# One diffusion step on one core: the low parts, the second Fourier pass and the modulation units moved between stages

## Chip, core and metric

The kernel runs on one core of a Trainium2 chip, as one launch. The metric is the device time of one execution in microseconds; lower is better. Five engines run their own instruction streams in order and wait for one another by semaphores: PE (TensorE, matrix products), ACT (ScalarE), DVE (VectorE), POOL (GpSimd) and SP (SyncE, which only issues transfers here).

## The reference, cut

One layer of a hybrid network is computed for 128 context tokens and 256 latent tokens (T = 384 columns in all), model width D = 2048, in float32:

```python
mod = jax.nn.silu(cond) @ lw['w_ada'] + lw['b_ada']            # 6 modulation vectors
h = rmsnorm(x, norm_pre_mix) * (1.0 + sc1) + sh1
proj = h @ lw['w_in']                  # q, k, v, output gate g, decay factors, Fourier groups fo
o = GLA(q, k, v, decays)               # 4 heads, chunks of 64, two directions
o = (o * rsqrt(mean(o * o)) * gla_out_norm * silu(g))
f = jnp.fft.fft2(fg, axes=(1, 3), norm='ortho').real           # 4 groups of 256 channels
gates = jax.nn.sigmoid(h @ lw['w_gate'] + lw['b_gate'])
merged = g_a * (o @ lw['w_br_gla']) + g_b * (f @ lw['w_br_four'])
m = merged @ lw['w_out']
x = x + ga1 * rmsnorm(m, norm_post_mix)
h = rmsnorm(x, norm_pre_ffn) * (1.0 + sc2) + sh2
ff = (silu(h @ w_ffn_gate) * (h @ w_ffn_up)) @ w_ffn_down
x = x + ga2 * rmsnorm(ff, norm_post_ffn)
```

## The kernel before

**Numbers in two parts.** PE multiplies in a rounded float32 format. To keep float32 accuracy each weight and each activation is split into a high part (the rounded value) and a low part (the rest), and each product is three matmuls: high with high, high with low, low with high. Weights come from HBM in granules of 128 rows by 1024 columns (512 KB). For each granule `load` issues the transfer into a `raw` buffer on SP's queue, and `split` makes the two parts: ACT casts `raw` to `whi` (lines 290, 293, 299, the same cast at three places), and then DVE subtracts, `wlo = raw - whi` (line 286). Four buffers of each part exist; granules are split about three ahead of their use. `grab` takes the next finished granule and then pushes one more load and split into the streams. The instructions of PE, ACT, DVE and POOL stay in the order in which the program is written; SP's transfers are ordered by a scheduler.

**Stages.** In order: the v projection with the first normalisation (to about 150 us); q, k and the first 25 of 32 branch-gate columns, with the GLA heads woven in (to 440 us); the last 7 gate columns with the Fourier channel transform woven in, the folding stage (to 544 us); the 8 output gates with the DFT over positions and the first Fourier projections woven in (to 665 us); the 16 GLA branch projections with the remaining Fourier projections (to 745 us); `w_out` (to 880 us); and the FFN. One 128-column projection is two halves, each 24 matmuls on one granule (`proj`, line 325).

**Work at the side.** After each half `proj` steps a side generator once. In the GLA stage (`side` at the GLA stage) that is one step of `gla` and one of the modulation; in the folding stage one turn of `run_after`; among the output gates one unit of modulation, one step of the DFT and one of the Nyquist weights.

**Modulation units.** The modulation vectors 2 to 4 come from `ada_rest`. One unit takes one 128 x 1024 block of `w_ada` (`adaw`, loaded on POOL's queue, two buffers) and adds it, scaled by one column of the conditioning for each of the two token kinds, to `adacc`: two DVE instructions (lines 704 and 706). Where `on_pe` is set, the unit is four matmuls into `pr` on PE instead (line 696). After 16 units of a vector half come a step without work, a step in which eight matmuls collect `adacc` into `pr` (line 717) and ACT copies it to `adev`, and a step in which PE transposes that into `ptm` (line 670) and DVE writes `mods`. What is left after the `w_out` column KT-4 is drained at once. `ada` is the same generator, slowed or quickened by `rate`. `TAIL` names the GLA branch projections that carry a unit, and whether it runs on PE.

**The folding stage.** It has 14 turns, one after each half. `ends` n adds mirrored token columns (DVE t, line 725; four r, lines 730 and 731; ACT casts the high part), `parts` n writes the low part of that (hF, line 737), and an `f` is one granule of Fourier columns against the folded activations: 16 matmuls into `pfo` (lines 1036 and 1037). Its granule is first combined in place by two DVE instructions (`fold_across`, raw, lines 255 and 256); such a granule's low part already waits until the next split (`low_due`), that of a gate granule follows its own cast at once. There are two passes of eight `f` each, for two pairs of groups; each pass fills four of the five PSUM buffers named `side`, and ACT and DVE copy the first pass's sums out (X, lines 1043 and 1044).

**The Fourier projections.** `four` i (17 matmuls into `pf`, lines 1233 to 1236) takes a granule of `w_br_four` that DVE first folds into `ws` (lines 243 and 244); its result is evicted by ACT (fd), combined by DVE (fd, y), multiplied by its gate and stored to DRAM, from where the GLA branch projection of the same column reads it back. In the stage of the output gates one `four` stands between the two halves of columns 3 to 7, and one after most columns. `gcol` finishes a column: three transposes (pt), ACT gs, DVE gs, ACT o_hi, DVE o_lo.

Of the kernel before, what the change touches and what calls it, by code (L numbers as in the profile page):

```python
# [22 lines left out]
KT = D // P  # L23
# [14 lines left out]
XU = 2  # L38
GF = 25
GD = 256  # L40
TAIL = {2: True, 5: True, 8: True, 11: False, 12: True, 13: False, 14: False}


C_TRI = 0
# [63 lines left out]
def tile_step(ctx: ExitStack, tc: tile.TileContext, a, o):  # L108
# [57 lines left out]
    turns = 2 * (32 - GF)  # L166
    after = [[] for _ in range(turns)]
    for n in range(8):
        at = n + n // 4
# [1 line left out]
        after[at + 1].insert(0, ("parts", n))  # L171
        after[at + 3].insert(0, ("f", 0, n))
    for n in range(8):
        after[turns - 1 - (7 - n + 1) // 4].append(("f", 1, n))
    across = set()
    for at, todo in enumerate(after):
        srcs.append(a["w_gate"][GF + at // 2, at % 2])
# [6 lines left out]
    fourier = iter(range(KT))  # L184
    mix_order = []
    between = [[] for _ in range(8)]
    for i in range(8):
        mix_order.append(("o", i))
        if i > 2:
            between[i].append(next(fourier))  # L190
            mix_order.append(("b", between[i][0]))
        mix_order += [("b", next(fourier)) for _ in range((i > 1) + (i == 7))]
    for i in range(KT):
        mix_order.append(("a", i))
        if i in (1, 4, 7, 9):
            mix_order.append(("b", next(fourier)))
    folded = set()
    for b, i in mix_order:
# [46 lines left out]
        return ws.rearrange("p i g c -> p (i g c)")  # L245

    folded_due = []
    low_due = []
    crossed = iter(range(KT))
    wq = const.tile([P, KT, 4], F32, name="wq")  # L250
# [12 lines left out]
    def split(at=None, eng=DVE, defer=None):  # L263


        if raws:
            raw, pairs, spare = raws.pop(0)
            if spare and depth[0] > 2:
                spare_raws.append(spare)
            if pairs == 2:  # L270
                fold_across(raw)
            while low_due:
                low_due.pop()()
            hi, lo = (
                p.tile([P, G], F32R, tag=t, name=n, bufs=b)
                for n, (p, t, b) in zip(("whi", "wlo"), at or ((wp, "whi", 4), (wp, "wlo", 4)))
            )
            for cast, _ in folded_due:
                cast()
            while folded_due:  # L280
                folded_due.pop()[1]()
            if pairs == 1:
                raw = fold(raw)

            def low():
                eng.tensor_sub(lo, raw, hi.bitcast(F32))  # L286
                ready.append((hi, lo))

            if pairs == 2:
                ACT.copy(hi, raw)  # L290
                low_due.append(low)
            elif pairs:
                folded_due.append((lambda: ACT.copy(hi, raw), low))
            elif defer is not None:
                ACT.copy(hi, raw)
                defer.append(lambda: eng.tensor_sub(lo, raw, hi.bitcast(F32)))
                ready.append((hi, lo))
            else:
                ACT.copy(hi, raw)  # L299
                low()  # L300

    def push():
        if not depth[0]:
# [57 lines left out]
    def catch_up():  # L361
        while later:
            later.pop()()
# [318 lines left out]
    on_pe = [False]  # L682
# [69 lines left out]
    with ExitStack() as s:  # L752
# [25 lines left out]
        def gla():  # L778
# [10 lines left out]
            for h in range(NH):  # L789
# [9 lines left out]
                for d in range(2):  # L799
                    s0.append(pg.tile([P, 1, DV], F32, tag=f"s0{d}", name="s0"))  # L800
                    SP.dma_start(s0[d], a["s0"][d, h])
                yield
                qin, kin, kcr, kout, dec = [], [], [], [], []

                z = [pss.tile([P, n, 2, P], F32, tag="side", name="z") for n in (2, 1)]
# [15 lines left out]
                split_act(lah, lal, la)  # L821
                yield
                if h == 0:
                    yield
                    yield
                for d in range(2):

# [138 lines left out]
        def side():  # L966
            while True:
                next(gl, None)
                next(ada, None)
                yield  # L970

        sd = side()
        for i in qk_order[1:]:
            proj(psm, hT, keep(qk, i), sd)

# [36 lines left out]
    with ExitStack() as s:  # L1012
# [33 lines left out]
        def run_after():  # L1046
            for at, todo in enumerate(after):
                for what, *n in todo:
                    if what == "ends":
                        ends(*n)  # L1050
                    elif what == "parts":
                        over_parts(2 * n[0], folds.pop(n[0]), True)
                    else:
                        if n == [1, 5]:
                            depth[0] = 2
                            spare_raws.clear()
                        across_n(*n)
                if at == turns // 2:
                    SP.dma_start(cd, a["consts"][:, C_CE:NC])
                if at == turns - 1:  # L1060
                    next(ada, None)
                yield

        ra = run_after()
        for i in range(GF, 32):
            proj(psm, hT, gate(more, i), ra)
            if i == GF:
                depth[0] = 4
                spare_raws.extend([lambda: more.tile([P, G], F32, tag="raw3", name="raw3", bufs=2)] * 2)
        catch_up()  # L1070
        depth[0] = 0
        xq = px.tile([P, HT], F32, name="xq")
        POOL.memset(xq, 0.0)
# [14 lines left out]
    with ExitStack() as s:  # L1088
# [84 lines left out]

        def side():
            while True:
                on_pe[0] = turn[0] > 5 and turn[0] % 2
                turn[0] += 1
                next(ada, None)
                on_pe[0] = False
                next(df, None)  # L1180
                next(nw, None)
                yield
# [71 lines left out]
        for b, i in mix_order:  # L1254
            if b == "o":
                if i == 1:
                    gate_of()
                proj(psm, hT, lambda p, i=i: gcol(p, i), sd, [lambda n=n: four(n) for n in between[i]])
                if i == 1:
                    gate_of()  # L1260
                continue
            if b == "b":
                if not i:
                    for g in (df, nw):
                        for _ in g:
                            pass
                    depth[0] = 4
                    spare_raws.extend([
                        lambda: px.tile([P, G], F32, tag="wr", name="raw3"), lambda: px.tile([P, G], F32, tag="cd", name="raw3"),
                    ])  # L1270
                if not any(i in x for x in between):
                    four(i)
            else:
                catch_up()
                if mT is None:
                    mT = alloc_A()
                if i == KT - 4:
                    depth[0] = 2
                    spare_raws.clear()
                if i in TAIL:  # L1280
                    on_pe[0] = TAIL[i]
                    next(ada, None)
                    on_pe[0] = False
                p = psm.tile([P, T], F32, tag="mm", name="pmm")
                w = grab()
                while unstored:
                    unstored.pop()()
                gemm(p, w, oT, 8)
                g, y = gates.pop((b, i))
                DVE.tensor_mul(g, g, p)  # L1290
                DVE.tensor_add(y, y, g)
                if late:
                    split_act(*late.pop())
                late.append((mT[0][:, i, :], mT[1][:, i, :], y))
                gate_of()
# [797 lines left out]
```

## Time and profile before

| what | value |
| --- | --- |
| time, median of 3 runs | 1955.1 us (1954.99 to 1955.59) |
| the profiled execution | 1954.77 us, of which its span 1953.0 us |
| busy in it: PE, DVE, ACT | 1924.9, 1653.2, 915.8 us |
| PE without work in the span | 28.1 us |
| mean granted TensorE clock | 0.997 |

The span runs from the first to the last recorded instruction; the other 1.8 us lie around it. A row of the timeline gives the start, the duration, the engine, the line and operation, output and inputs, and in brackets how long the engine sat idle before it and what ended that. A row of the windows gives, for a stretch of the span, its length and the busy time of PE, PE's weight loads, DVE, ACT and POOL with their instruction counts, then the granted clock, the DMA share and GB/s. PE sums overlapping matmuls only once, so a stretch in which PE is busy throughout still can be slower than another.

### The profile page before, as it was taken

The page shows a single profiled execution, that of the slowest core. Times are in us where ns is not written, and L with a number is a line of the kernel's source. Part 1 is how long each engine was busy: PE and PEld are TensorE (multiplying, and loading weights), DVE is VectorE, ACT ScalarE, POOL GpSimd, SP SyncE. Part 2 cuts the span into 40 slices and gives each one's busy share as a digit, 9 for nine tenths or more (in the row PEclk, how much of TensorE's full clock was granted, in tenths as well). Part 3 has the DMA queues.
Part 4 walks back from the last instruction along what each step waited for, and adds up shares of the span by engine and source line. Part 5 has one row for each costly group of instructions (what it writes and reads, how often), then busy time and mean ns, then how long its engine had stood idle before and what let it go on. Part 6 is the DMA issues. An engine that isn't in the chain of part 4 may idle for free.

```text
span 1953.0 us, 27519 instructions
## 1 busy us (share of the span) xinstructions
PE 1924.9 (99%) x10518; PEld 1693.6 (87%) x10518; DVE 1653.2 (85%) x2176; ACT 915.8 (47%) x1298; POOL 85.8 (4%) x154
## 2 busy tenths in 40 slices
PE   8999999999999999999999999999999999999997
PEld 5779999999999899999988888888888888888886
DVE  5668798888878987987789898998998999887885
ACT  4235445544446654456455444444444444444454
POOL 0001110100000000104000000000000000000001
PEclk9999999999999999999999999999999999999999
DMA  9976766766657885656254535363636263625243
GB/s 390 381 269 237 253 225 234 233 230 200 188 178 234 304 294 202 215 204 223 84 170 151 185 117 185 126 207 109 205 117 207 92 222 99 201 68 192 86 170 111
DMA packets 200615, 380.52 MB, mean 195 GB/s; under 512 B 14196, under 2 KB 126932, under 8 KB 196132
## 3 DMA queue, kind: packets, MB, share of 16 engines
q1 hardware_dynamic: 181396, 321.83, 48.5%
q0 software_dynamic: 13952, 50.39, 8.3%
q10 hardware_dynamic: 5136, 6.56, 0.9%
q8 instruction: 82, 1.34, 0.3%
q14 instruction: 49, 0.40, 0.1%
HBM read 361.94 MB, written 16.78 MB: 194 GB/s over the span
## 4 chain that ended last, share of the span: by engine, by line
PE 88%; DVE 5%; DMA 2%; ACT 2%; issue 1%; SPq 0%; ACTq 0%; DVEq 0%
PE pgu L337 30%; PE pmm L325 28%; PE pdn L337 18%; PE pv L490 3%; PE pgm L473 1%; PE pfo L1036 1%; DVE wlo L286 1%; PE pmm L1510 1%; DMA slab<-in_w_ada 1%; ACT whi L299 1%; PE ptr L1802 1%; DMA raw<-in_w_in 1%; DMA xraw<-in_w_x 1%; PE po L787 1%; DVE adacc L706 0%
## 5 line engine op out<-in xcount | busy, mean ns | idle before, releaser
L325 PE MATMUL pmm<-A_hi,whi 128*128 128x384 f32 x1072 | 361.5, 337 | 0.0
L325 PE MATMUL pmm<-A_lo,whi 128*128 128x384 f32 x1072 | 358.6, 335 | 0.0
L325 PE MATMUL pmm<-A_hi,wlo 128*128 128x384 f32 x1072 | 358.6, 334 | 0.0
L1657 ACT CAST whi<-u 128x1024 fp32r<-128x1024 f32 x200 | 210.6, 1053 | 273.1 <-DVE u L1641 83.9
L1657 ACT CAST whi<-raw 128x1024 fp32r<-128x1024 f32 x175 | 184.2, 1052 | 208.8 <-DMA raw<-in_w_g 66.2
L1668 DVE TENSOR_TENSOR wlo<-u,whi 128x1024 fp32r<-128x1024 f32 x200 | 244.2, 1221 | 28.5 <-ACT whi L1657 16.7
L337 PE MATMUL pgu<-whi,A_hi 128*128 128x512 f32 x640 | 250.0, 391 | 0.0
L337 PE MATMUL pgu<-whi,A_lo 128*128 128x512 f32 x640 | 249.3, 389 | 0.0
L1668 DVE TENSOR_TENSOR wlo<-raw,whi 128x1024 fp32r<-128x1024 f32 x175 | 213.5, 1220 | 34.7 <-ACT whi L1657 23.5
L286 DVE TENSOR_TENSOR wlo<-raw,whi 128x1024 fp32r<-128x1024 f32 x163 | 198.0, 1221 | 40.8 <-ACT whi L299 37.3
L299 ACT CAST whi<-raw 128x1024 fp32r<-128x1024 f32 x149 | 155.9, 1050 | 118.4 <-PE pmm L325 47.6
L706 DVE SCALAR_TENSOR_TENSOR adacc<-adaw,spad,adacc 128x1024 f32<-128x1024 f32 x164 | 203.0, 1279 | 1.5 <-DMA adaw<-in_w_ada 1.3
L325 PEld LDWEIGHTS pmm<-A_hi,whi 128*128 128x128 f32 x1072 | 201.2, 188 | 2.9 <-issue 2.1
L325 PEld LDWEIGHTS pmm<-A_lo,whi 128*128 128x128 f32 x1072 | 201.4, 188 | 0.2
L325 PEld LDWEIGHTS pmm<-A_hi,wlo 128*128 128x128 f32 x1072 | 201.2, 188 | 0.0
L337 PE MATMUL pdn<-whi,hid_hi 128*128 128x512 f32 x480 | 186.9, 389 | 0.0
L337 PE MATMUL pdn<-whi,hid_lo 128*128 128x512 f32 x480 | 186.8, 389 | 0.0
L337 PE MATMUL pgu<-wlo,A_hi 128*128 128x512 f32 x640 | 184.2, 389 | 0.0
L337 PEld LDWEIGHTS pgu<-whi,A_hi 128*128 128x128 f32 x640 | 120.1, 188 | 26.1 <-issue 0.8
L337 PEld LDWEIGHTS pgu<-wlo,A_hi 128*128 128x128 f32 x640 | 120.2, 188 | 25.4
L337 PEld LDWEIGHTS pgu<-whi,A_lo 128*128 128x128 f32 x640 | 120.1, 188 | 25.0
L337 PE MATMUL pgu<-whi,S 128*128 128x512 f32 x480 | 131.1, 395 | 0.0
(405 smaller groups left out, 3050.6 us busy)
## 6 DMA issues: line engine op xcount, KB each, us to landing
adaw<-in_w_ada POOLq DMA_DIRECT2D x96, 512.0 KB, 3.9
raw<-in_w_d SPq DMA_DIRECT2D x88, 512.0 KB, 3.8
slab<-in_w_ada SPq DMA_DIRECT2D x32, 1024.0 KB, 9.8
raw<-in_w_gate SPq DMA_DIRECT2D x64, 512.0 KB, 4.5
raw<-in_w_g SPq DMA_DIRECT2D x48, 512.0 KB, 3.8
raw<-in_w_u SPq DMA_DIRECT2D x48, 512.0 KB, 3.8
raw<-in_w_in SPq DMA_DIRECT2D x44, 512.0 KB, 4.1
u<-in_w_u SPq DMA_DIRECT2D x40, 512.0 KB, 4.7
```

The costliest lines, as they stand in the source:

```text
L286: eng.tensor_sub(lo, raw, hi.bitcast(F32))
L299: ACT.copy(hi, raw)
L325: PE.matmul(dst, w[wi][:, k * n + n0 : k * n + n0 + P], x[xi][:, k0 + k, :], start=first and k == 0 and j == 0, stop=last and k == kts - 1 ...
L337: PE.matmul(dst, stat[x_][m], mov(w[w_], m), start=first and w_ == m == x_ == 0, stop=last and w_ == m == 1,)
L473: PE.matmul(pgv[q : q + 32, :], spad[:, k, :], slab[k // (KT // 2)][:, k % (KT // 2), :], start=k < 4, stop=k >= KT - 4,)
L490: PE.matmul(pv[2 * t + g], hT[x_][:, kb, t * P : (t + 1) * P], w_[:, g * 512 : (g + 1) * 512], start=kb == 0 and j == 0, stop=kb == KT - 1 ...
L706: DVE.scalar_tensor_tensor(acc[:, c, :], w, spad[:, k, c : c + 1], acc[:, c, :], op0=ALU.mult, op1=ALU.add,)
L787: PE.matmul(dst, w[wi], x[xi], start=first and j == 0, stop=last and j == 2)
L1036: PE.matmul(p, w_of[0][:, i, k, g, :], x[:, :, lo:hi], start=kt == 0, stop=False)
L1510: PE.matmul(hp[u], hw[u][j][:, ((k - 1) % 8) * P : ((k - 1) % 8 + 1) * P], h2[m][:, k - 1, :], start=k == 1 and j == m == 0, stop=k == KT ...
L1657: ACT.copy(hi, src)
L1668: DVE.tensor_sub(lo, src, hi.bitcast(F32))
```

## The change

It alters where five kinds of work stand; what is computed stays the same.

```diff
-TAIL = {2: True, 5: True, 8: True, 11: False, 12: True, 13: False, 14: False}
+TAIL = {1: True, 4: False, 5: True, 8: True, 10: False, 11: True, 14: False}
+RATE = 1.07
...
     for n in range(8):
-        after[turns - 1 - (7 - n + 1) // 4].append(("f", 1, n))
+        after[turns - 2 + n // 4].append(("f", 1, n))
...
-        mix_order += [("b", next(fourier)) for _ in range((i > 1) + (i == 7))]
+        mix_order += [("b", next(fourier)) for _ in range(i > 1)]
...
-        if i in (1, 4, 7, 9):
+        if i in (0, 3, 6, 9, 12):
...
                 ACT.copy(hi, raw)
-                low()
+                low_due.append(low) if low_later[0] else low()
...
                     SP.dma_start(s0[d], a["s0"][d, h])
                 yield
+                if h == 0:
+                    yield
...
                 if h == 0:
-                    yield
                     yield
...
         sd = side()
+        rate[0] = RATE
...
-                if at == turns - 1:
-                    next(ada, None)
+                if at in (turns - 4, turns - 3, turns - 1):
+                    next(ada_gen, None)
...
         ra = run_after()
+        low_later[0] = True
...
         catch_up()
+        low_later[0] = False
...
-                on_pe[0] = turn[0] > 5 and turn[0] % 2
+                on_pe[0] = turn[0] > 5
+                if turn[0] < 6 or turn[0] % 2:
+                    next(ada_gen, None)
+                on_pe[0] = False
                 turn[0] += 1
-                next(ada, None)
-                on_pe[0] = False
...
-                if i == KT - 4:
+                if i == KT - 3:
                     depth[0] = 2
                     spare_raws.clear()
                 if i in TAIL:
                     on_pe[0] = TAIL[i]
-                    next(ada, None)
+                    next(ada_gen, None)
```

In words: in the folding stage the low part of a gate granule is subtracted one granule later. The second pass has its eight `f` in turns 12 and 13 (four each), where one stood in turn 11, four in turn 12 and three in turn 13. Modulation: 1.07 units for each of the 60 half steps of the GLA stage after the first column (1.0 before), three units in the folding stage (one before), and among the output gates units in the first six turns and in the odd ones after, these on PE (one in every turn before); the seven of `TAIL` move, four on PE and three on DVE as before. In GLA's first head the matmuls into z stand one half later, with one half less after them, and one `four` goes from the output gates to the GLA branch projections, where five now stand, after columns 0, 3, 6, 9 and 12.

DVE in the early turns of the folding stage, before (names as in the words above; x2 is two in a row):

```order
L286 TENSOR_TENSOR wlo<-raw,whi 128x1024 x2
L737 TENSOR_TENSOR hF<-r,hF 128x2x384
L725 TENSOR_TENSOR t<-A_hi,A_lo 128x768
L730 TENSOR_TENSOR r<-t 128x2x64
L731 TENSOR_TENSOR r<-t 128x2x63
L730 TENSOR_TENSOR r<-t 128x2x128
L731 TENSOR_TENSOR r<-t 128x2x127
L255 TENSOR_TENSOR raw_4601<-raw_4601 128x2x256
L256 SCALAR_TENSOR_TENSOR raw_4601<-raw_4601 128x2x256
L737 TENSOR_TENSOR hF<-r,hF 128x2x384
L286 TENSOR_TENSOR wlo<-raw_4601,whi 128x1024
```

And now:

```order
L288 TENSOR_TENSOR wlo<-raw,whi 128x1024
L739 TENSOR_TENSOR hF<-r,hF 128x2x384
L727 TENSOR_TENSOR t<-A_hi,A_lo 128x768
L732 TENSOR_TENSOR r<-t 128x2x64
L733 TENSOR_TENSOR r<-t 128x2x63
L732 TENSOR_TENSOR r<-t 128x2x128
L733 TENSOR_TENSOR r<-t 128x2x127
L257 TENSOR_TENSOR raw_4617<-raw_4617 128x2x256
L258 SCALAR_TENSOR_TENSOR raw_4617<-raw_4617 128x2x256
L288 TENSOR_TENSOR wlo<-raw,whi 128x1024
L739 TENSOR_TENSOR hF<-r,hF 128x2x384
L288 TENSOR_TENSOR wlo<-raw_4617,whi 128x1024
```

The gate granule's wlo, the second of the pair at the top before, has moved behind one hF, the t, the r and the two raw; the other rows keep their order, and a wlo now stands between a raw pair and hF.

PE where the first pass ends and the second begins (turn 11), before, with the buffers' numbers, since they tell the passes apart (pfo_468x is the first pass, pfo_520x the second):

```order
L1036 MATMUL pfo_4684<-hF_4517,whi_5083 128x388
L1037 MATMUL pfo_4684<-hF_4517,wlo_5084 128x194
L1036 MATMUL pfo_4685<-hF_4517,whi_5083 128x380
L1037 MATMUL pfo_4685<-hF_4517,wlo_5084 128x190
L1036 MATMUL pfo_5203<-hF_4514,whi_5119 128x388
L1037 MATMUL pfo_5203<-hF_4514,wlo_5120 128x194
```

And now, where 24 matmuls of a half follow the first pass (its first three are shown) before pfo_526x begins:

```order
L1040 MATMUL pfo_4700<-hF_4533,whi_5099 128x388
L1041 MATMUL pfo_4700<-hF_4533,wlo_5100 128x194
L1040 MATMUL pfo_4701<-hF_4533,whi_5099 128x380
L1041 MATMUL pfo_4701<-hF_4533,wlo_5100 128x190
L327 MATMUL pmm_5227<-A_hi_92,whi_5132 128x384
L327 MATMUL pmm_5227<-A_lo_93,whi_5132 128x384
L327 MATMUL pmm_5227<-A_hi_92,wlo_5133 128x384
```

The first half of the last gate column stands between the passes.

DVE among the output gates, turn 6, before:

```order
L1246 TENSOR_TENSOR y<-y,gate 128x384
L243 TENSOR_TENSOR ws<-raw_5875 128x512
L244 TENSOR_TENSOR ws<-raw_5875 128x512
L706 SCALAR_TENSOR_TENSOR adacc<-adaw,spad,adacc 128x1024 x2
L286 TENSOR_TENSOR wlo<-ws,whi 128x1024
L286 TENSOR_TENSOR wlo<-raw_5877,whi 128x1024
```

And now:

```order
L1253 TENSOR_TENSOR y<-y,gate 128x384
L244 TENSOR_TENSOR ws<-raw_5909 128x512
L245 TENSOR_TENSOR ws<-raw_5909 128x512
L288 TENSOR_TENSOR wlo<-ws,whi 128x1024
L288 TENSOR_TENSOR wlo<-raw_5911,whi 128x1024
```

The two adacc of that turn are gone from DVE; the same holds for turns 10, 12 and 14.

More of the change, by code (lines that the diff above doesn't have):

```diff
@@ L247, in tile_step @@
     folded_due = []
+    low_later = [False]
     low_due = []
```

## The prediction

> **What bounds the kernel now.** I read the page's busy times and chain first, then the waits of PE, then busy time and granted clock by stage, then the rows of DVE and PE around each wait. The chain of waits that ended last, by engine:
>
> ```profile
> PE 88%; DVE 5%; DMA 2%; ACT 2%; issue 1%; SPq 0%; ACTq 0%; DVEq 0%
> ```
>
> PE sets the end. The change adds almost nothing to PE and removes nothing, so it can win only what PE now loses in the stages it touches. PE's waits there, from the list of waits:
>
> ```profile
> PE pf L1234 <- DVE wlo L286: 3.4, 4, 1.5
> ...
> PE pfo L1036 <- DVE X L1044: 1.8, 1, 1.8
> PE z L807 <- ACT krs L795: 1.4, 1, 1.4
> PE ptm L670 <- ACT adev L666: 1.0, 1, 1.0
> PE pfo L1037 <- DVE wlo L286: 0.8, 1, 0.8
> PE pfo L1036 <- ACT whi L290: 0.8, 1, 0.8
> ```
>
> That is 9.2 us, in nine waits. The windows show where, and that some of them cost twice (GLA, folding, folding again, output gates, their end):
>
> ```profile
> 165.00:440.00 275.00, 275.00 (x1790) 270.69 (x1789) 239.60 (x304) 133.58 (x232) 29.82 (x59) 1.00 0.69 233
> 486.00:516.00 30.00, 26.59 (x152) 25.45 (x151) 25.43 (x37) 14.53 (x25) 0.00 (x0) 0.94 0.54 171
> 492.00:504.00 12.00, 10.38 (x53) 9.80 (x52) 10.54 (x15) 6.64 (x10) 0.00 (x0) 0.86 0.34 111
> 580.00:665.00 85.00, 81.60 (x526) 76.50 (x525) 77.32 (x143) 49.92 (x78) 5.28 (x10) 0.99 0.74 245
> 660.00:672.00 12.00, 10.52 (x54) 10.22 (x54) 10.86 (x24) 9.85 (x16) 0.00 (x0) 0.86 0.96 340
> ```
>
> Folding loses 30.00 - 26.59 = 3.4 us to idle time and the output gates 85.00 - 81.60 = 3.4. The granted clock is 1.00 through all of GLA, but 0.86 over 12 us after the two folding waits of 0.8 and again after the 1.5 us wait: (1 - 0.86) x 12 = 1.7 us more, twice. All that the change can reach is 3.4 + 1.7 + 3.4 + 1.7 + 1.4 + 1.0 = 12.6 us, 0.6% of the time.
>
> **GLA: the z step and four more units.** Moving z back by a half (4.2 us of matmuls, row below) covers a wait of 1.4: it goes. The chain behind it keeps its place, since the half is taken from the two spare ones after it. Rate 1.07 over 60 half steps adds four units. A unit occupies DVE 596.75 - 594.36 = 2.4 us (rows among the output gates, below), four 9.6; DVE's idle time in GLA is 275.00 - 239.60 = 35 us, and PE idles nowhere in it. In the new order the doubled steps stand in the light end of a head (po steps) and never right ahead of a lal. The last one, just ahead of the folding stage, has this beside it:
>
> ```profile
> 433.46 1.23 DVE L286 TENSOR_TENSOR wlo<-raw,whi 128x1024 fp32r<-128x1024 f32 x1 [1.64 <-ACT whi L299]
> 435.93 0.23 DVE L939 RECIPROCAL rs<-rs 128x12 f32<-128x12 f32 x1 [1.24 <-ACT rs L938]
> ```
>
> 1.64 + 1.24 = 2.9 us of DVE waiting takes up 2.4. So: -1.4, and nothing for the units; if that cover is gone, up to 2.4 us late into folding.
>
> **Folding: low parts later.** One full turn of DVE (with a row from the stage's start), and what PE has meanwhile, from the timeline and the chain (an f, then a half, whose third matmul is the first to use a wlo):
>
> ```profile
> 445.27 1.22 DVE L286 TENSOR_TENSOR wlo<-raw,whi 128x1024 fp32r<-128x1024 f32 x1
> ...
> 488.91 0.95 DVE L737 TENSOR_TENSOR hF<-r,hF 128x768 fp32r<-128x768 f32 x1
> 489.78 0.95 DVE L725 TENSOR_TENSOR t<-A_hi,A_lo 128x768 f32<-128x768 f32 x1
> ...
> 491.85 0.69 DVE L255 TENSOR_TENSOR raw<-raw 128x512 f32<-128x512 f32 x1
> ...
> 493.18 0.95 DVE L737 TENSOR_TENSOR hF<-r,hF 128x768 fp32r<-128x768 f32 x1
> 494.43 1.23 DVE L286 TENSOR_TENSOR wlo<-raw,whi 128x1024 fp32r<-128x1024 f32 x1 [0.30 <-ACT whi L290]
> 496.41 1.23 DVE L286 TENSOR_TENSOR wlo<-raw,whi 128x1024 fp32r<-128x1024 f32 x1 [0.76 <-ACT whi L299]
> 497.55 0.95 DVE L725 TENSOR_TENSOR t<-A_hi,A_lo 128x768 f32<-128x768 f32 x1
> ```
>
> ```profile
> 456.54 0.34 PE L1036 MATMUL pfo<-hF,whi 128*128 128x388 f32 x1
> ...
> 458.81 0.36 PE L325 MATMUL pmm<-A_hi,whi 128*128 128x384 f32 x1
> 459.00 0.33 PE L325 MATMUL pmm<-A_lo,whi 128*128 128x384 f32 x1
> 459.17 0.34 PE L325 MATMUL pmm<-A_hi,wlo 128*128 128x384 f32 x1
> ```
>
> ```profile
> 458.97 4.21 PE pmm L325 x24
> ```
>
> From t to t DVE needs 7.77 us, 1.06 of it waiting for casts that were ordered just before; PE needs 2.27 + 4.21 = 6.48. DVE therefore slips over 1 us per full turn until PE stands still. With the gate's wlo behind the next raw pair both casts have been made when DVE comes to them: 6.71 a turn, and only three turns are full; turn 7 has no f, turns 4 and 9 to 11 no t. So the two 0.8 us waits and the clock behind them go. The 1.8 us wait for X goes by itself: a half of 4.21 us now lies between the passes. The two units added in turns 10 and 11 (4.8 us) fall in turns without t, r and hF (491.85 - 489.78 + 0.87 = 2.9 us each, 5.9).
>
> The deferral also has a price. Laying the new rows end to end from the end of qk at 445.27, where the wlo of the row above began (t, r and raw 3.40, wlo 1.14, hF 0.87), the wlo of the half that PE starts at 458.81 ends at 445.27 + 3.40 + 1.14 + 0.87 + 2.07 + 1.14 + 0.87 + 3.40 + 1.14 = 459.3; PE wants it with its third matmul, at 459.2. The two are level; before, that subtraction came t, r, raw and hF earlier (4.3 us). The bounds are 0 and 0.5 (level again a turn later); I take +0.3, since both sums agree within 0.2. Folding: -3.4 - 1.7 + 0.3 = -4.8.
>
> **Output gates: units off DVE.** Of 16 units DVE loses those of turns 6, 10, 12 and 14; one of the odd ones, on PE, is new:
>
> ```profile
> 586.81 0.61 DVE L1193 SCALAR_TENSOR_TENSOR gs<-gs,gnorm,pt 128x384 f32<-128x384 f32 x1
> ...
> 588.95 1.23 DVE L286 TENSOR_TENSOR wlo<-ws,whi 128x1024 fp32r<-128x1024 f32 x1 [0.39 <-ACT whi L293]
> ...
> 591.23 0.62 DVE L1238 TENSOR_TENSOR fd<-fd,pf 128x194 f32<-128x194 f32 x2
> ...
> 593.16 0.69 DVE L243 TENSOR_TENSOR ws<-raw 128x512 f32<-128x512 f32 x1
> ...
> 594.36 2.47 DVE L706 SCALAR_TENSOR_TENSOR adacc<-adaw,spad,adacc 128x1024 f32<-128x1024 f32 x2
> 596.75 1.22 DVE L286 TENSOR_TENSOR wlo<-ws,whi 128x1024 fp32r<-128x1024 f32 x1
> ...
> 610.96 1.23 DVE L286 TENSOR_TENSOR wlo<-ws,whi 128x1024 fp32r<-128x1024 f32 x1 [1.17 <-ACT whi L293]
> ```
>
> ```profile
> 590.23 0.36 PE L1234 MATMUL pf<-edT,wlo 128*128 128x194 f32 x1 [0.63 <-DVE wlo L286]
> ...
> 627.75 0.42 PE L1233 MATMUL pf<-edT,whi 128*128 128x388 f32 x1
> ...
> 630.22 0.36 PE L325 MATMUL pmm<-A_hi,whi 128*128 128x384 f32 x1
> ```
>
> ```profile
> 641.12 0.64 PE L696 MATMUL pr<-adaw,spad 128*32 128x256 f32 x8
> 641.69 0.55 PE L1190 MATMUL pt<-ident,qk 128*128 128x128 f32 x3
> 641.99 0.42 PE L1233 MATMUL pf<-edT,whi 128*128 128x388 f32 x1
> ```
>
> The first wait (0.63) comes of the units of turns 4 and 5, which stay: the rows from the adacc of turn 4 to that wlo are the same, so it stays. The other three go if DVE keeps up. Two turns of DVE without a unit: two wlo twice (4 x 1.14), fd and y twice (593.16 - 591.23 = 1.93), ws twice (1.20), the wait for the cast once (1.17), gs to wlo once (588.95 - 586.81 = 2.14): 14.1 us. PE: two halves (8.42), two four (630.22 - 627.75 = 2.47), pr (0.57), pt (0.30): 14.2. With a unit DVE needs 16.5. So DVE no longer falls behind, with next to no slack; after 590.23 its lead is the 0.4 to 0.8 us that the missing unit of turn 6 leaves (596.75 - 2.39 + 1.17 = 595.5, ending 596.7, against a need at 597.3). I take the three waits and the clock as gone: -(3.4 - 0.6) - 1.7 = -4.5. The bounds are 0 and -5.1. The extra unit on PE: +0.6. At the end of the stage one four instead of two in a row spares DVE 1.93 + 1.20 + 1.14 = 4.3 us and PE 2.5. The five four among the GLA branches are spread by three products, and PE had no wait in that stage.
>
> **w_out.** One unit more is done ahead of it, so in the new order the eight pr stand 24 matmuls ahead of the ptm at the drain, and the wait of 1.0 for adev goes: -1.0.
>
> **Sum.** -1.4 - 4.8 - 4.5 + 0.6 - 1.0 = -11.1 us. The profiled execution took 1954.77 (span 1953.0, 1.8 around it), 0.3 below the median of the runs: 1955.1 - 11.1 = **1944.0 us**. At the best bounds (no price in folding, the first pf wait gone too) it is -12.0. The idle figures may also be short: PE counts as busy through a matmul's modelled 0.36 us, while the next could start 0.19 later (459.00 - 458.81), so each of nine waits may hide 0.17 us, 1.5 in all: 1941.6 at best.
>
> **The clock, by row and by rule.** The rows show 0.86 granted after two waits of 0.8 us. The Trainium skill, page "TensorE: Matmul & The Clock Gate", section "What's actually happening", has the clock fall to half only after an idle window of about 3.4 us, and its section "Why this matters for your kernels" warns of gaps above about 3 us. By that, gaps of at most 1.8 us cost no clock, and the dips would have another cause and stay; by the Trainium skill's rule the sum would end at 1947.4, the second rival's time. The trace disagrees with it: GLA, with no gap, has 1.00 throughout, and the dips stand right behind the waits.
>
> **Rivals.**
> 1. Folding keeps its loss: the units of turns 10 and 11 and the blocks of four f make DVE late for the second pass (a granule there costs DVE 1.33 + 1.14 = 2.47 against PE's 2.27). For it: the level sum above. Against: three granules stand ready. Price: the 4.8 come back, 1948.8. 12%.
> 2. The clock falls for another reason than the waits: 3.4 come back, 1947.4. 8%.
> 3. The output gates stay bound by DVE (14.1 against 14.2 leaves no room for a wait on ACT): their 4.5 come back, 1948.5. 10%.
> 4. Slower: DVE is the bound wherever a unit is added. Place: the doubled GLA steps and folding turns 10 and 11. It decides once a unit exceeds DVE's idle time beside it. Then 4 x 2.4 + 2 x 2.4 = 14.4 lie on the path, folding gains nothing, the rest (-1.4 - 4.5 + 0.6 - 1.0 = -6.3) stays: +8.1, 1963.2. For it: DVE at 25.43 of 30.00 in folding. Against: 35 us idle in GLA. 7%.
> 5. The change doesn't do what it says: each wait appears a granule later, and only z and ptm are won: -1.4 - 1.0 + 0.6 = -1.8, 1953.3. 8%.
>
> **Chances and range.** The forecast has 55%. About 0.2% (3.9 us) is what a measurement of this kernel tells from no change. The forecast and rivals 1 to 3 lie beyond it: faster 85%; rival 5 is within it, 8%; slower 7%. The range runs from the best sum less the spread between the runs shown (0.6) and half a microsecond for the semaphores themselves, which no row prices, 1940.5, to the near side of rival 5, 1953.0.
>
> **What would show it.** Right: no idle PE in z; none at pfo and granted clock 1.00 between 486 and 540; one pf wait of about 0.6, not four; no clock dip after 655; ptm without a wait; DVE's wlo in folding no longer waiting for whi L299. Wrong: a pmm waiting for wlo in turns 4 and 5, pfo of the second pass waiting for wlo, pf waits at each even turn, or a bT held up by lal in GLA. A loss anywhere in w_out or the FFN would make the prediction wrong in a place that I left at zero.

## The result, and the profile after

| | before | after |
| --- | --- | --- |
| median of 12 runs each | 1954.95 us (1952.83 to 1955.59) | 1954.76 us (1952.94 to 1961.19) |
| ratio, 95% interval | | 1.0003 (0.9994 to 1.0012) |
| span of the profiled execution | 1953.0 us | 1953.0 us |

No change that can be measured; the forecast was 11.1 us less. In one experiment below, e6, one of seven executions took 3884 us: the median given there includes it, the ratio does not. The list of PE's waits of the kernel after, longest first:

```profile
PE pmm L327 <- DVE wlo L288: 4.2, 2, 3.7
PE py L1950 <- DVE ep L2008: 1.8, 1, 1.8
PE at L875 <- DVE ki L852: 1.8, 1, 1.8
PE pr L719 <- DVE adacc L708: 1.5, 2, 0.9
PE bT L835 <- DVE lal L380: 0.9, 2, 0.6
PE ptr L1809 <- DVE ep L1802: 0.7, 1, 0.7
PE pf L1241 <- DVE wlo L288: 0.7, 1, 0.7
```

Eight of the nine waits that the prediction listed are gone, as it said: all three at pfo, z, ptm, and three of four at pf. New ones stand in their place, and all of them are for DVE: at pmm, at, pr and bT, and at ptr in the FFN (py was there before). The windows of after, by stage (length, busy time and count of PE, weight loads, DVE, ACT and POOL, granted clock, DMA share, GB/s) show where they are:

```profile
165.00:440.00 275.00, 270.84 (x1765) 266.19 (x1764) 245.93 (x309) 135.03 (x234) 31.93 (x63) 1.00 0.70 238
440.00:486.00 46.00, 42.28 (x236) 41.78 (x235) 41.37 (x65) 18.48 (x30) 4.60 (x8) 0.93 0.65 219
486.00:516.00 30.00, 30.00 (x186) 30.00 (x185) 27.39 (x39) 13.85 (x23) 0.80 (x2) 1.00 0.61 191
580.00:665.00 85.00, 84.34 (x544) 79.94 (x543) 70.55 (x134) 53.01 (x82) 3.69 (x7) 1.00 0.69 229
```

GLA, where PE never stood still in this stretch, now loses 4.2 us. The folding stretch from 486 is clean, as forecast, but the one ahead of it, which had PE busy for all of its 46.00 us, loses 3.7 and part of its clock. The output gates lose 0.7 instead of 3.4.

PE's starts of its first matmul into pfo, pfq (right behind folding) and pst (right behind w_out) cut the span into four parts. The third and fourth columns are after minus before, forecast and measured; the last is e11, a kernel of the experiments below, minus before:

| part | before | forecast | after | e11 |
| --- | --- | --- | --- | --- |
| to the first pfo (GLA) | 456.54 | -1.4 | +2.85 | -0.67 |
| pfo to pfq (folding) | 84.73 | -4.8 | +1.40 | -5.19 |
| pfq to pst (output gates, branches, w_out) | 340.94 | -4.9 | -5.79 | -5.79 |
| pst to the end (FFN) | 1070.8 | 0 | +1.5 | +0.3 |

So 5.8 us were won behind folding and given back in three places. Against the forecast, 4.3 us are missing in GLA, 6.2 in folding and 1.5 in the FFN, which the change does not touch; the third part won 0.9 more than forecast.

**Folding.** Its loss is one half, the fifth, that PE starts at 461.78. Rows of PE, DVE, ACT and SP of after around it:

```profile
462.06 0.34 PE L327 MATMUL pmm<-A_lo,whi 128*128 128x384 f32 x1
466.12 0.69 PE L327 MATMUL pmm<-A_hi,wlo 128*128 128x384 f32 x1 [3.71 <-DVE wlo L288]
```

```profile
451.71 1.22 DVE L288 TENSOR_TENSOR wlo<-raw,whi 128x1024 fp32r<-128x1024 f32 x1
...
458.98 0.29 DVE L733 TENSOR_TENSOR r<-t 128x126 f32<-128x126 f32 x1
462.84 0.43 DVE L732 TENSOR_TENSOR r<-t 128x256 f32<-128x256 f32 x1 [3.57 <-ACT r L728]
```

```profile
460.68 1.05 ACT L301 CAST whi<-raw 128x1024 fp32r<-128x1024 f32 x1 [3.89 <-DMA raw<-in_w_gate]
...
462.61 0.20 ACT L728 COPY r<-t 128x4 f32<-128x4 f32 x1 [0.40 <-ACT gz L983]
```

```profile
449.32 1.57 SPq L1063 DMA_DIRECT2D cd<-in_consts  x1
453.00 0.33 SPq L235 DMA_DIRECT2D raw<-in_w_gate  x1
```

```profile
452.16 1.15 POOL L692 DMA_DIRECT2D adaw<-in_w_ada  x2
```

Read from the bottom up. SP issues the gate granule's transfer at 453.00, right when the deferred wlo (451.71 to 452.85) lets its raw buffer go, and behind the load of constants cd and POOL's loads, the last of them two blocks of `w_ada` of 512 KB. From 453 to 461 the windows give a DMA share of 1.01 at 357 GB/s: the DMA engines are busy throughout. ACT's cast waits for the transfer until 460.68, 7.7 us after its issue. ACT works in order, so r stands behind that cast, DVE's next r behind ACT's r, and the wlo that PE wants behind DVE's r. DVE is not short of time here: it stands idle for 3.57 us. The clock pays a second time; the windows of PE (granted clock, DMA share, GB/s at the end):

```profile
464.00:468.00 4.00, 1.88 (x6) 0.62 0.19 47
468.00:472.00 4.00, 4.00 (x15) 0.53 0.65 215
472.00:476.00 4.00, 4.00 (x28) 1.00 0.42 132
```

The half takes 10.84 us from start to start instead of 4.21. Of the 6.6 us more, 3.9 lie between two matmuls' starts that are otherwise 0.17 apart (the wait of 3.71 is counted from a modelled end), and 2.7 come of the lower clock.

**GLA.** PE's and DVE's rows of after in the first head:

```profile
223.98 0.64 PE L719 MATMUL pr<-adacc,selr 128*32 128x256 f32 x8 [0.91 <-DVE adacc L708]
225.18 0.64 PE L719 MATMUL pr<-adacc,selr 128*32 128x256 f32 x8 [0.56 <-DVE adacc L708]
```

```profile
187.41 1.22 DVE L288 TENSOR_TENSOR wlo<-raw,whi 128x1024 fp32r<-128x1024 f32 x1
188.55 0.55 DVE L851 SCALAR_TENSOR_TENSOR qi<-eb,qk 128x384 f32<-128x384 f32 x1
189.02 0.55 DVE L852 TENSOR_TENSOR ki<-ki,qk 128x384 f32<-128x384 f32 x1
...
222.64 2.48 DVE L708 SCALAR_TENSOR_TENSOR adacc<-adaw,spad,adacc 128x1024 f32<-128x1024 f32 x2
```

The same ki before:

```profile
188.77 0.55 DVE L849 TENSOR_TENSOR ki<-ki,qk 128x384 f32<-128x384 f32 x1
```

PE starts its first matmuls into `at` at 187.38 and waits 1.8 us for the ki of 189.02. From 182 to 225 DVE works almost without a pause, and the same rows stood there before, 0.2 us earlier. PE's time won at z only brought it sooner to a DVE that was no sooner. The wait at pr has another cause: the first doubled step of the new rate takes the blank step and pr at once, so pr comes one half sooner after the unit of 222.64 (before, the unit stood at 222.42 and pr at 228.00).

### The profile page after: what moved, and what is told of

The parts are those of the page before. It is cut to its first block, busy times and chain, and to the rows that moved or that the text cites. A ratio compares the mean times of both kernels' runs of the same rounds, so it can differ in the third digit from the quotient of the medians.

```text
span 1953.0 us, 27535 instructions
## 1 busy us (share of the span) xinstructions
PE 1923.8 (99%) x10526; PEld 1692.8 (87%) x10526; DVE 1650.9 (85%) x2174; ACT 915.7 (47%) x1298; POOL 85.8 (4%) x154
## 3 DMA queue, kind: packets, MB, share of 16 engines
q8 instruction: 82, 1.34, 0.3%
## 4 chain that ended last, share of the span: by engine, by line
PE 71%; DVE 3%; DMA 1%; ACT 1%; issue 0%; ACTq 0%; DVEq 0%; SPq 0%
PE pgu L339 30%; PE pdn L339 18%; PE pmm L327 17%; PE pf L1240 1%; PE pmm L1517 1%; PE pfo L1040 1%; PE ptr L1809 1%; PE pf L1241 1%; DMA raw<-in_w_d 0%; DMA raw<-in_w_gate 0%; PE pfo L1041 0%; DVE adacc L708 0%; DVE x1b L1961 0%; DMA raw<-in_w_in 0%; PE pr L698 0%
```

## The experiments

The experiments ran in three groups, each with the kernel before beside it; its median was 1954.5 to 1954.6 in all three, and ratios are against it. Each kernel has one profile; those of e8 and e10 are of their slowest executions, 4.6 and 4.5 us above their medians.

**e1: the first low part not deferred.**

```diff
-        low_later[0] = True
         for i in range(GF, 32):
             proj(psm, hT, gate(more, i), ra)
             if i == GF:
+                low_later[0] = True
                 depth[0] = 4
```

> The change, but the deferral of low parts is switched on only after the first gate column of the folding stage: one wlo, of the first gate granule there, goes back ahead of t. Theory A (buffers): until that column is done only two raw buffers exist, and the deferred wlo (451.71 to 452.85) holds one; the transfer of the granule used at 461.78 is issued at 453.00 and lands at 460.68. Then the 3.7 us wait for wlo goes and with it the slow half behind it (10.84 us instead of 4.21): 6 us less, about 1948.5. Theory B (order on DVE): the wlo of that granule is late because it stands behind t, r, raw and hF, which it still does here: the wait stays above 2.5 us and the time at 1954. Theory C (DVE late out of GLA by the added units): wait and time stay.

1949.47 us, ratio 0.9976 (0.9968 to 0.9985). The transfer is issued at 450.13 together with its neighbour and ahead of cd, and the wait is 0.55, with the clock at 1.00:

```profile
463.01 0.45 PE L327 MATMUL pmm<-A_hi,wlo 128*128 128x384 f32 x1 [0.55 <-DVE wlo L288]
```

One wlo in another place is worth 5.3 us. Theories B and C fall as the cause of the 3.7. B explains the 0.55 that is left: in e1 that granule's wlo begins at 461.74 and ends 14.0 us after the first wlo of the stage (448.88), the sum that the prediction laid end to end from 445.27 to 459.3. But DVE reaches the stage 3.6 us later than before, and PE 3.1.

**e2: four raw buffers from the start.**

```diff
         low_later[0] = True
+        depth[0] = 4
+        spare_raws.extend([lambda: more.tile([P, G], F32, tag="raw3", name="raw3", bufs=2)] * 2)
         for i in range(GF, 32):
             proj(psm, hT, gate(more, i), ra)
-            if i == GF:
-                depth[0] = 4
-                spare_raws.extend([lambda: more.tile([P, G], F32, tag="raw3", name="raw3", bufs=2)] * 2)
```

> The change, with the deferral in every turn, but with the two extra raw buffers and the depth of four granules from the first turn of the folding stage instead of after its first column. The order of the low parts on DVE is that of the change. Theory A: transfers no longer wait for a deferred wlo, the 3.7 us wait goes, about 1948.5. Theories B and C: nothing changes for DVE, the wait stays above 2.5 us, 1954 to 1955. Either way the earlier transfers may meet others in the first turns: up to 1 us.

1951.94 us, ratio 0.9993 (0.9984 to 1.0002; two of eleven runs lie 4 us above the rest). The wait is 2.64. By the numbers alone that speaks for B, but DVE's row says what it waited for:

```profile
452.07 0.69 DVE L257 TENSOR_TENSOR raw<-raw 128x512 f32<-128x512 f32 x1 [2.32 <-DMA raw<-in_w_in]
```

The gate granule was in time (its cast follows at 458.38 with no wait); now the Fourier granule ahead of it came late, its transfer issued only at 447.63. A transfer again, but another one: the run doesn't tell A from B cleanly, and the time lies between their forecasts.

**e3: one unit per half step in GLA.**

```diff
-RATE = 1.07
+RATE = 1.0
```

> The change with one unit of modulation per half step of GLA, as before (four fewer there; they are left for the drain in w_out). Theory A, with the units as the cause of GLA's waits: pr for adacc (1.5 us) and bT for lal (0.9) go, at for ki (1.8) stays because it is the wait at z moved on; the 3.7 us wait in folding stays; w_out loses about 1 us at ptm and up to 2 more for four units drained: 1953 to 1955. Theory C: DVE comes out of GLA earlier by up to 4.8 us, so the folding wait falls below 1 us and the time to about 1948. If the at wait goes too, it was the units' and not the z step's.

1960.88 us, ratio 1.0037 (1.0023 to 1.0050). The waits at pr (1.5 us) and bT are gone, and the first pfo comes at 456.43 instead of 459.39: the added units cost 3.0 us in GLA. The wait at at stays (1.34): that one belongs to the z step. The folding wait stays at 3.72, though DVE and PE are 3 us earlier: theory C falls. The four units that were left over cost more at the drain in w_out than was expected, 8.0 us in one wait:

```profile
PE pr L719 <- DVE adacc L708: 8.0, 1, 8.0
PE pmm L327 <- DVE wlo L288: 4.0, 2, 3.7
```

**e5: the constants later.**

```diff
                 if at == turns // 2:
+                    DVE.memset(cd[:, 0:1], 0.0)
                     SP.dma_start(cd, a["consts"][:, C_CE:NC])
```

> The change, with the 967 KB load of constants (cd) held back to turn 7 by a DVE instruction of one column ahead of it, so that it is no longer between the gate transfers of 448.78 and 453.00. If that load makes the transfer issued at 453.00 land late (7.7 us after issue, against a median of 5.4 in that stretch and 3.6 to 4.6 over the page), it lands about 3.5 us earlier and the wait of 3.7 falls to 0 to 0.7: about 1949 to 1950. If only the late buffer counts (theory A alone) or the order on DVE (B) or GLA (C), the wait stays above 2.5 us and the time at 1954.

1951.28 us, ratio 0.9987 (0.9978 to 0.9996). The granule's cast starts at 459.07 instead of 460.68, and the wait is 2.60: issued at 452.7, the transfer took 6.4 us instead of 7.7 without the load of constants ahead of it, and 1.1 of the 3.7 are that load's share. Neither forecast holds: the wait is not gone, and the time is not 1954. Why it still took 6.4 is not shown. POOL's loads are still there (four into `wr`, two into `adaw`, issued from 449.6 to 452.5), and the DMA share from 452.7 to 459 is 0.85; no run moves them away.

**e6: z where it was.** From here on the edits are made on e1, but for e8 and e12.

```diff
                     SP.dma_start(s0[d], a["s0"][d, h])
                 yield
-                if h == 0:
-                    yield
...
                 if h == 0:
                     yield
+                    yield
```

> The kernel of e1 (first low part not deferred), with the matmuls into z of GLA's first head back where they stood before the change. Theory Z1 (DVE is the bound in head 0, without a pause of over 1 us from 161 to 227 us): the wait of 1.4 at z returns, the wait of 1.6 at the at matmuls goes, the time stays at that of e1, 1949.5, within 0.7. Theory Z2 (the wait at the at matmuls comes of the added units, the z step did win its 1.4): it stays at about 1.6, z waits 1.4 again, 1950.9.

1948.78 us, ratio 0.9971 (0.9960 to 0.9982), within the scatter of e1. Z1: z waits 1.44, at nothing, and the first pfo comes at 459.24 (459.66 in e1). The z step wins nothing while DVE is the bound behind it.

**e7: the second pass where it was.**

```diff
-        after[turns - 2 + n // 4].append(("f", 1, n))
+        after[turns - 1 - (7 - n + 1) // 4].append(("f", 1, n))
```

> The kernel of e1, with the second pass where it stood before the change (one f right behind the first pass). If the half between the passes hides the eviction, as forecast: a wait of about 1.8 for X returns and the granted clock falls behind it, 1.8 to 3.5 us slower than e1, 1951.3 to 1953.0. If the eviction is hidden by something else now: 1949.5 and no wait for X. If DVE is the limit there, a wait for wlo stands in its place.

1948.68 us, ratio 0.9971 (0.9962 to 0.9980), no wait for X. The 1.8 us before was not the price of passes that follow each other at once. ACT's rows of before, then of e7:

```profile
512.94 1.04 ACT L290 CAST whi<-raw 128x1024 fp32r<-128x1024 f32 x1 [0.58 <-DVE raw L256]
513.89 0.97 ACT L1043 COPY X<-pfo 128x194 f32<-128x194 f32 x4
```

```profile
512.05 1.17 ACT L1047 COPY X<-pfo 128x194 f32<-128x194 f32 x4 [0.56 <-PE pfo L1041]
```

Before, X stood on ACT behind a cast that waited for a late DVE. With DVE in time, ACT copies X as soon as the sums are there. By the profiles, moving the second pass even costs a little: e1 has a wait of 0.54 at pmm in it, e7 none, and folding takes 80.23 and 79.77 us.

**e8: no deferral at all.** An edit of the change itself:

```diff
-        low_later[0] = True
         for i in range(GF, 32):
```

> The change without any deferral of low parts; second pass, units, z and output gates as changed. The deferral's own worth, as forecast: the two waits of 0.8 at pfo return in turns 6 to 9, with the granted clock at 0.86 behind them, 3.3 us in all, and against e1 the waits of 0.55 and 0.54 go: about 1951.7. If DVE, later out of GLA than before, has no lead, the waits are longer than before (2 to 3 us in all): 1953. Rival: the deferral wins nothing, its waits only move: 1949 to 1950, as e1.

1958.69 us, ratio 1.0027 (1.0015 to 1.0038), 9 us above e1, more than expected. In its profile folding takes 88.61 us, against 80.23 in e1: waits of 0.81 and 0.81 around 504 and of 3.20 in the second pass at 531, with the clock down behind the pair and behind the third:

```profile
PE pfo L1041 <- DVE wlo L288: 4.2, 3, 3.2
PE pfo L1040 <- ACT whi L292: 0.8, 1, 0.8
```

Without the deferral folding takes 84.73 us in the kernel before and 88.61 here. The units are one difference between the two (one in the stage and three), but not the only one: the second pass and DVE's start into the stage differ too. The profile also has a wait of 3.1 us in GLA's last head, behind a gate transfer that ACT waited for, as that of e10 has one of 2.3; no edit explains these two, and it may be they that put these two executions above their medians.

**e9 and e11: the units of GLA set by half step.** `ada_gen` is the generator without a rate; `CALLS` names the half steps of GLA (numbered from the first) that take none or two, for e9 and e11:

```diff
-RATE = 1.07
+CALLS = {4: 0, 5: 0, 13: 2, 14: 2, 17: 0, 18: 2, 27: 2, 29: 2, 41: 2, 43: 2, 44: 2}
...
-RATE = 1.07
+CALLS = {4: 0, 14: 2, 16: 2, 28: 2, 35: 2, 49: 2}
...
-        rate[0] = RATE
...
-            while True:
+            for s in range(1000):
                 next(gl, None)
-                next(ada, None)
+                for _ in range(CALLS.get(s, 1)):
+                    next(ada_gen, None)
                 yield
```

e9 also leaves out the unit of turn 5 among the output gates.

> The kernel of e1, with the units of modulation set by half step: none in steps 4 and 5 of GLA (ahead of the first head's at matmuls), one moved behind the second head's lal, doubled in steps 13, 14, 27, 29, 41, 43 and 44 (light ends of heads), none doubled ahead of the folding stage (65 steps of modulation in all, 64 in the change), and one unit less among the output gates, that of turn 5. If the waits of GLA are DVE's lag at its due points: at 1.6, pr 1.5, bT 1.0 go, folding's 0.55 too since DVE comes out of GLA 2.4 us earlier, and the pf wait of 0.7: up to 5 us, 1944.5 to 1946. If the added units cost DVE time wherever they stand: the waits only move, 1949 to 1950, and the bT waits of heads 2 and 3 are longer than 0.7.

e9: 1952.33 us, ratio 0.9995 (0.9986 to 1.0004). Slower than e1, and outside both forecasts. The wait at the first head's at, folding's at 462 and the last pf wait are gone, and pr in the first head waits 0.5 us. But at waits 1.3 us near 258, pr 1.5 near 306 and pmm 1.3 near 532, and the doubled steps 41 to 44 stand right ahead of a pr. PE's and DVE's rows:

```profile
383.69 1.85 PE L719 MATMUL pr<-adacc,selr 128*32 128x256 f32 x12 [4.08 <-DVE adacc L708]
```

```profile
375.77 2.48 DVE L708 SCALAR_TENSOR_TENSOR adacc<-adaw,spad,adacc 128x1024 f32<-128x1024 f32 x2 [3.29 <-DMA adaw<-in_w_ada]
```

DVE itself waits there for adaw, which has two buffers: units close together outrun their own transfers. That cost was in no theory.

> The kernel of e1, with 64 steps of modulation in GLA as in the change, but none in step 4 (ahead of the first head's at), and doubled in steps 14, 16, 28, 35 and 49, each behind a stretch without units or with the blank step between the last adacc and its pr kept; none doubled in the last ten steps. In e9 the double steps stood right ahead of a pr, which waited 4.1 us for adacc. Theory: a unit costs PE nothing where DVE has no due point (ki, lal, adacc for pr) within two half steps: the waits at 1.6, pr 1.5 and bT 0.6 of 1.0 go, and folding's 0.55: 1945 to 1946.5. Rival: DVE has no room left beside GLA at all, the waits only move: 1949 or more, with waits of 3 us or more in GLA.

e11: 1943.87 us, ratio 0.9947 (0.9935 to 0.9960), faster than before and after both, and about 1 us below its forecast. Its list of PE's waits from 160 to 700 us:

```profile
PE pf L1241 <- DVE wlo L288: 0.7, 1, 0.7
PE bT L835 <- DVE lal L380: 0.6, 2, 0.4
PE dl L789 <- DVE part L380: 0.5, 1, 0.5
PE pmm L327 <- DVE wlo L288: 0.2, 1, 0.2
```

64 steps of modulation in both, and 5.6 us less than e1. By the profiles 3.8 us of that lie in GLA and 0.7 in folding, which are the units' doing: what a unit costs depends on where it stands. The rest lies in the FFN (below).

**e10: the output gates' modulation as before.**

```diff
-                on_pe[0] = turn[0] > 5
-                if turn[0] < 6 or turn[0] % 2:
-                    next(ada_gen, None)
+                on_pe[0] = turn[0] > 5 and turn[0] % 2
+                next(ada_gen, None)
```

> The kernel of e1, with the modulation among the output gates as before the change (a unit in every turn, on PE at the odd turns from 7 on; four DVE units more). If these units were what made PE wait at pf, as forecast: three more waits of 0.8 to 1.5 come back, with the slow clock behind the last, and one unit on PE goes (0.6): 4 us slower than e1, about 1953.5. If the output gates were short of something else (a cast, a transfer): within 1 us of e1.

1952.71 us, ratio 0.9994 (0.9985 to 1.0003). From pfq to pst it takes 339.89 us, e1 335.16: 4.7 us, in six waits of 0.7 at pf where e1 has one. The forecast for these gates (3.9 with the unit on PE) holds, though the waits are more and shorter than expected and no slow clock follows them:

```profile
PE pf L1240 <- DVE wlo L288: 4.1, 6, 0.7
```

**e12: the kernel before with the deferral alone,** from the second column of folding on, as in e1:

```diff
+    low_later = [False]
...
-                low()
+                low_due.append(low) if low_later[0] else low()
...
             if i == GF:
+                low_later[0] = True
...
         catch_up()
+        low_later[0] = False
```

> The kernel before, with nothing changed but the deferral of low parts in the folding stage, from its second column on (as in e1). No unit is added ahead of the stage or in it, and the second pass stands as before. The folding loss of 3.4 us of waits and 1.7 of clock then goes, 5 us: 1949.5 to 1950. If the deferral only pays beside the added units: 1953 or more. If the wait of 1.8 for X is the second pass's own, and not DVE's being late, it stays: 1951.5.

1947.74 us, ratio 0.9967 (0.9955 to 0.9979): one edit alone wins 6.9 us, where 5 were expected. Folding, window by window, has neither idle time nor a slow clock:

```profile
486.00:516.00 30.00, 30.00 (x189) 30.00 (x188) 25.33 (x36) 15.29 (x26) 0.00 (x0) 1.00 0.58 173
516.00:545.00 29.00, 29.00 (x241) 27.71 (x241) 21.92 (x25) 13.69 (x24) 0.63 (x2) 1.00 0.63 197
```

It takes 79.00 us, 5.7 less than before, and the wait for X is gone without the second pass having been moved. By the profiles 1.6 us more are won between pfq and pst, where this edit changes nothing: the clock did not fall behind the wait of 1.48 there (last section).

## Why the prediction was wrong

Three of the signs that the prediction named as showing it wrong are there: a pmm that waits for wlo early in folding, a bT held up by lal in GLA, and a loss in the FFN.

**z, -1.4.** Wrong as a gain by itself. The wait went, and came back as 1.8 at at (e6: the two kernels are equal). The step said that the chain behind z keeps its place; it looked at PE's halves and not at DVE, which was the bound from 182 to 225.

**Four units in GLA, "nothing for the units".** This is one of the two steps that failed. Its cover was DVE's 35 us of idle time in the whole stage, and an order without doubled steps right ahead of a lal. e3 measured the price: 3.0 us, at pr and bT and 0.4 of the wait at at. The sum of idle time was there (e11 does as many steps for nearly nothing), but not where the units stood. The sum counted one kind of due point, lal, and not the adacc that pr takes, nor ki; and the 0.9 at bT is a wait for lal all the same.

**Folding, -3.4 - 1.7 for the low parts.** Right. e1 won 4.5 us from pfo to pfq against 4.8 forecast, e12 5.7.

**Price of the deferral, +0.3.** The other step that failed; it cost 5.3 us (e1 against the change). The sum for DVE was right to a tenth, as e1 shows, but it followed one engine. A raw buffer that is held one granule longer starts the next transfer later, with only two buffers until the first column is done, and ACT's cast, ACT's r and DVE's r queue behind that transfer. The bounds of 0 to 0.5 left the queue of SP out. What is shown is that this deferral makes the transfer late and that the late transfer costs this; why the transfer then took as long as 7.7 us is shown for 1.3 of it only (e5).

**The second pass.** The wait for X went, but not by the half between the passes: e7 and e12 lose it without that half. The size was right, by luck as far as the step goes: its cause was wrong.

**Two units in folding, for nothing.** Nearly right where the low parts are deferred: folding takes 79.54 us with three units (e11) and 79.00 with one (e12). Without the deferral it takes 3.9 us more with three (e8) than with one (before), but other edits differ there too, so the units' share is not shown.

**Output gates, -4.5, and +0.6 for PE.** Right: 4.7 by e10 against 3.9, the one wait of 0.66 left at pf, no slow clock behind 655.

**w_out, -1.0.** Right: ptm has no wait.

**Rivals.** Rival 4 was right that units cost DVE's time in GLA, but at due points and for 3 us, not 9.6. Rival 5 came near the time (1953.3) by another road: the waits did not move a granule on, a transfer was late. Rivals 1 and 3 did not come: the second pass waits 0.5 us in after, and the output gates won. Rival 2, another reason for the clock, has nothing for it: in the thirteen profiles no window of 4 us between 156 and 956 us had a granted clock below 0.97 without a wait of PE ahead of it. The half microsecond for semaphores in the lower end of the range stands on no row of any run.

Where both failed steps are mended the sum comes out: e11 takes 1943.9 us, forecast 1944.0. It has the change's units but for the half steps that they stand in, and its deferral but for one granule. That it agrees to 0.1 us is partly luck: by parts it wins 0.7 us less than forecast in GLA, and 0.4 and 0.9 more in the next two.

**The FFN, 0.** In the thirteen profiles, pst to the end takes 1070.8 to 1074.0 us. The seven kernels that have both the rate of 1.07 and the changed output gates (after, e1, e2, e5 to e8) take 1072.2 us or more, the six others 1071.1 or less. The loss stands near the end, in six of the seven at ptr, which waits 0.7 us for ep. Each has one profile, and how work so far ahead could reach there is open; 1.5 us of the miss lie here.

## What to carry to other kernels

Before you let a buffer go later, ask which transfer starts from it and follow that transfer through every queue that will wait for it; the engine that does the deferred work may stand idle meanwhile. Idle time of an engine summed over a stage is no cover: place added work by the due points behind it (what it delays within the next two steps, and whether its own loads come fast enough). When a wait goes, look at what the next engine does in that time; if it has no pause there, the wait only moves on.

## What the runs showed of the hardware

A single wait of 2.6 us (e5, in folding) was enough to lower the granted clock:

```profile
464.00:468.00 4.00, 3.50 (x12) 0.57 0.48 143
```

In the thirteen profiles, from 160 to 900 us, so did every longer one (2.64, 3.2, 3.7, 4.1 and 8.0 us), the 2.3 of e10 and the 3.1 of e8, each with 0.7 more behind it, and the two of 0.8 before, 1.3 us apart. Single waits up to 1.44 us never did, nor did 0.9 and 0.6, 1.2 us apart, at pr in after. Between 1.48 and 2.1 us both outcomes occur. At the first head's at, where these kernels are alike up to there, the clock fell behind waits of 1.73 (e5; 0.67 from 192 to 196) and 1.95 (e8; 0.68), and stayed at 1.00 behind 1.64 (e1), 1.76 (after) and 2.1 (e7). One wait of 1.48 us for the same wlo had both outcomes, here before and in e12, where the kernel is the same behind folding:

```profile
664.00:668.00 4.00, 4.00 (x19) 0.67 0.98 308
```

```profile
656.00:660.00 4.00, 3.64 (x24) 1.00 0.86 268
660.00:664.00 4.00, 4.00 (x25) 1.00 1.01 349
```

Counting 1.7 us of clock for each such place, as the prediction did, therefore takes one outcome of a chance for its price. The Trainium skill, page "TensorE: Matmul & The Clock Gate", section "What's actually happening", has the clock judged in a window of 3.4 us that runs free of the program. That the window runs free would fit the two outcomes of one wait, which is argued and not shown; that it takes an idle window of 3.4 us does not fit the single waits of 1.48, 1.73 and 2.6 that lowered the clock here.

In the FFN's last part, ahead of that ptr, a granule's cast began 3.5 us after its transfer was issued before (1885.27 to 1888.79), and 5.1 after (1883.77 to 1888.83); why is open.
